# Where two modulation vectors are summed in a two-block diffusion transformer kernel

## The chip, the cores and the metric

The kernel runs on one core of a Trainium2 chip. The metric is the device time of one execution in microseconds (us). Three runs of the kernel before took 2163.9, 2153.99 and 2159.36 us; the median is 2159.36 us. One more execution was profiled; its own time is 2165.34 us and its traced span 2163.6 us.

The engines go by these names: PE is TensorE (matmuls; PEld are its weight loads), DVE is VectorE, ACT is ScalarE, POOL is GpSimd, and SP is SyncE, whose queue issues nearly all transfers of this kernel.

## The reference

Everything is fp32. 256 tokens and 256 context tokens of width 1024 pass through a first block of two layers and a second block of one layer; each layer is a mixer and then routed experts. The inputs of both halves are scaled and shifted, and their outputs gated, by six vectors that are computed from a condition:

```python
for layer in range(DEPTH):
    w_ada, b_ada = ada_w[layer], ada_b[layer]
    mod = (jax.nn.silu(c) @ w_ada + b_ada)[:, None, :]
    mod_c = (jax.nn.silu(c_ctx) @ w_ada + b_ada)[None, None, :]
    sh1, sc1, g1, sh2, sc2, g2 = jnp.split(mod, 6, axis=-1)
    csh1, csc1, cg1, csh2, csc2, cg2 = jnp.split(mod_c, 6, axis=-1)
    h = rms_norm(x, norm_mix_g[layer]) * (1.0 + sc1) + sh1
    ...
    x = x + g1 * y
    h2 = rms_norm(x, norm_ffn_g[layer]) * (1.0 + sc2) + sh2
    ...
    x = x + g2 * f[:b_ * t_].reshape(b_, t_, d_)
```

Here y is the mixer's output and f that of the experts. In layer 0 the mixer is an HGRN2 scan (4 heads) beside a differential attention (4 heads); the router picks 2 of 16 experts for each of the 512 tokens. Layer 1 has a windowed attention and the same kind of experts. The second block (another attention, a linear recurrence and 32 smaller experts) is not touched by the change.

The six vectors have the numbers 0 to 5 in the kernel: sh1, sc1, g1, sh2, sc2, g2. Vector 2 is the gate on the mixer's output, which is used when that output is projected; vector 5 is the gate on the experts' output, which is used from the experts' first scatter on.

## The kernel before, in words

`body` runs the six stages one after the other: `mixer0`, `moe(0)`, `mixer1`, `moe(1)`, `mixer2`, `moe(2)`. The code says what is computed and which tiles are shared; a scheduler then gives each engine one fixed row of instructions, mostly in the order in which the code reaches them, moved where it expects an operand late. An engine works through its row and waits at each instruction until its operands and its output buffer are free. SP does so too, so a transfer that waits for a page buffer holds up all transfers behind it.

**A modulation vector** is made by `ada(ps, parts, which, (v,))` in two halves (chunks) of 512 columns. For each, `ada_chunk` fetches two pages of 1 MB (4 of the 8 row blocks of the weight each), does 8 matmuls (L244, each 2 hardware instructions) into the four 32-row groups of one PSUM tile, and copies that to SBUF (L247: on DVE for the first chunk, on ACT for the second). `ada` then transposes the copy in 4 blocks (L265, 8 hardware instructions), and DVE adds up the four row groups (L267) and the bias (L269). Pages lie in 6 buffers, `pg`, that the weights of projections and experts share.

**mixer0** has a list of calls that lays the work of several heads in each other: H(h) is the next piece of HGRN2 head h, F(h) of attention head h, `a0(v)` and `a1(v)` are a modulation vector of layer 0 or 1. The last ones of before are H3, H3, H3, `a0(5)`, F3, F3, `a1(0)`, F3, `a1(2)`. A head's scan is a cascade of seven levels; at each, PE does 4 products (L453, 8 hardware instructions) and DVE three steps (L455, L457, L460). F3 ends in a softmax chain between PE (L546 scores, L563 transposes, L567 values), ACT and DVE. After the list, `router_start` folds vector 4 into the router's weights (L642), `as_row` spreads the gate over the partitions (L285), the output weights `even_w_out` (4 pages) are each split into a high and a low part (ACT L355, DVE L356), and `out_proj` multiplies (L366), gates (L581), adds (L584) and calls `router` for each of 4 token tiles: two transposes (L669, copies L670), the logits (L674) and L (L675).

**moe(0)** starts with the routing: DVE works out a mask `M` of the chosen experts; PE counts with it (L1349 to L1353), then spreads vector 5 by `as_row` (L285 again) and gathers tokens (L1499). Meanwhile ACT normalises the tokens (L1746, L1747) and POOL takes their low parts (L1748). At the end, `finish(1)` scatters the last 128 slots: for each of 8 half tiles, PE multiplies (L1567), DVE gates into a tile `t` (L1226; two buffers), and POOL or DVE adds to the tokens (L1571). Then every engine loads a count of overflowing blocks (`overflow`, L1868) and branches on it (L1874; the branch is taken past the body, as nothing overflows here). **mixer1** begins behind the branch with the norm of the tokens (ACT L295, transposes L327).

Of the kernel before, what the change touches and what calls it, by code (L numbers as in the profile page):

```python
# [20 lines left out]
P = 128  # L21
# [137 lines left out]
class K:  # L159
# [74 lines left out]
    def ada_chunk(self, ps, which, j, parts):  # L234

        nc, I = self.nc, self.I
        w = I["ada_w"][which] if which < 2 else I["w_ada_2"]
        s = 0 if which < 2 else 1
        wt = self.page(w[j])
        pa = self.t(ps, [P, 512], "ad", bufs=1) if which == 2 and j >= 4 else self.t(ps, [P, 512], "mm")  # L240
        for kk in range(2):
            for g in range(4):
                k = g + 4 * kk
                nc.tensor.matmul(out=pa[32 * g:32 * g + 32, :], lhsT=self.st[:, s, k, :],  # L244
                                 rhs=wt[:, k, :], start=(kk == 0), stop=(kk == 1))
        pt = self.w2(parts, [P, 512]) if which == 2 and j >= 4 else self.t(parts, [P, 512], "part")
        (nc.scalar.copy if j % 2 else nc.vector.tensor_copy)(out=pt, in_=pa)  # L247
        return pt
# [5 lines left out]
    def ada(self, ps, parts, which, vecs):  # L254
# [4 lines left out]
        for v in vecs:  # L259
            for half in (range(2) if isinstance(v, int) else (v[1],)):  # L260
                v = v if isinstance(v, int) else v[0]
                pt = self.ada_chunk(ps, which, 2 * v + half, parts)
                pc = self.t(ps, [P, 4, P], "tp")
                for b in range(4):
# [412 lines left out]
    def mixer0(self):  # L677
        tc, nc, I = self.tc, self.nc, self.I
        with ExitStack() as st:
# [53 lines left out]

            for f, v in ((H, 0), (H, 0), (H, 0), (H, 0), (a0, 2), (dval, 0), (F, 0), (F, 0), (H, 1), (F, 0), (H, 1), (H, 1), (H, 1), (a0, 4), (F, 1), (F, 1), (H, 2), (F, 1), (a1, 1), (H, 2), (H, 2), (H, 2), (a0, 3), (F, 2), (F, 2), (H, 3), (F, 2), (H, 3), (H, 3), (H, 3), (a0, 5), (F, 3), (F, 3), (a1, 0), (F, 3), (a1, 2)):
                f(v)
# [9 lines left out]
            for half in range(2):  # L745
                w = self.page(I["even_w_out"][half])
                wo.append(self.split(A, w, ("wh", "vt" if half else "wh"), (3, 1 if half else 3)))
            self.out_proj(ps, A, self.split_y(A, yT, ("hT0", "hT1")), wo, range(4), g1, 0, x0=x0)


# [949 lines left out]
    def moe(self, layer, plan, npages):  # L1700
# [6 lines left out]
        with ExitStack() as st:  # L1707
# [112 lines left out]
            for i, r in enumerate(rounds):  # L1820
# [4 lines left out]
                for p, ne in r:  # L1825
# [15 lines left out]
                    if layer == 1 and p == 1:  # L1841
                        self.early2(self.t(M, [P, 512], "t"))
            finish(1)
            slo, end, nbl = self.beyond(G, oh, info, nt, E, plan, ob)
            self.overflow(s, G, slo, end, nbl, E, ob, srcs, xtile)
# [144 lines left out]
```

## Time and profile before

| | |
|---|---|
| Median of three runs | 2159.36 us |
| The profiled execution: its time, its span | 2165.34 us, 2163.6 us |
| PE busy | 1946.4 us, 90% of the span |
| DVE, ACT, POOL busy | 941.3 (44%), 548.6 (25%), 248.0 us (11%) |
| Moved by transfers | 632.6 MB, 292 GB/s over the span |
| mixer0, and the routing after it | 0 to 464 us, to about 488 us |
| moe(0): experts, last scatter | about 488 to 1058 us, to 1073 us |
| mixer1, moe(1) | 1073 to about 1300 us, to about 1720 us |
| mixer2, moe(2) | to about 1900 us, to the end |

Busy shares are means over stages that differ: PE has no gap for long stretches and then waits for whole chains of other engines at the ends of a mixer and of the experts. What a piece of work costs is to be read at its place. A row of a timeline gives start and length in us, engine, line, operation, the tiles as output<-inputs, the shape, the count xN, and in brackets the idle time of the engine before it with what ended that. A row by line has the count, then busy us and mean ns of one, then the idle time before them and what ended it.

### The profile page before, as it was taken

How to read it: one execution, taken by the hardware profiler on the slowest of the kernel's cores; microseconds unless marked ns; L12 is line 12 of the kernel's file. 1: busy time of each engine (PE TensorE's matmuls, PEld its weight loads, DVE VectorE, ACT ScalarE, POOL GpSimd, SP SyncE). 2: the span in 40 equal slices, each digit the busy share in tenths (PEclk: the TensorE clock that was granted, in tenths of full speed). 3: DMA queues.
4: the chain of work that ended last, by engine and by line, in shares of the span. 5: the costliest groups of instructions: out<-in, count | busy, mean ns of one | idle time of the engine just before them, and what ended most of it. 6: DMA issues, size and time to landing. Idle time of an engine off the chain costs nothing. (4 is left out here: it accounts for less than half of the span.)

```text
span 2163.6 us, 29541 instructions
## 1 busy us (share of the span) xinstructions
PE 1946.4 (90%) x11795; PEld 1011.6 (47%) x11795; DVE 941.3 (44%) x2121; ACT 548.6 (25%) x1009; POOL 248.0 (11%) x203
## 2 busy tenths in 40 slices
PE   6999999969999999999799989998878869979986
PEld 3776665755443443333265563333322246655432
DVE  5536546454463234432456653222211155655533
ACT  4333433332221111110244431010100045521110
POOL 0000000020031012121300000101000011012212
PEclk9999999989999999999899999999999989989998
DMA  8423325335989998899554579999999976669997
GB/s 316 151 86 122 144 85 213 118 117 225 358 354 374 388 353 325 335 346 405 194 184 157 178 291 407 421 421 420 421 421 421 421 273 236 273 245 372 406 421 297
DMA packets 95587, 632.60 MB, mean 292 GB/s; under 512 B 15440, under 2 KB 17488, under 8 KB 19920
## 3 DMA queue, kind: packets, MB, share of 16 engines
q1 hardware_dynamic: 93888, 626.21, 73.5%
q10 hardware_dynamic: 1552, 4.39, 0.5%
q8 instruction: 97, 1.59, 0.3%
q14 instruction: 50, 0.41, 0.0%
HBM read 629.51 MB, written 1.05 MB: 291 GB/s over the span
## 5 line engine op out<-in xcount | busy, mean ns | idle before, releaser
L1602 PE MATMUL gu<-pg,xT 128*64 128x512 f32 (+1 forms) x2560 | 487.5, 597 | 19.5 <-DMA pg<-in_moe_gu_dram 19.5
L1635 PE MATMUL py<-pg,hT 128*64 128x512 f32 (+1 forms) x1280 | 258.3, 596 | 20.5 <-DVE hT L1619 17.4
L1602 PEld LDWEIGHTS gu<-pg,xT 128*64 128x64 f32 (+1 forms) x2560 | 133.1, 124 | 287.3 <-issue 231.1
L1571 POOL TENSOR_TENSOR xs<-xs,t 128x512 f32<-128x512 f32 x110 | 142.3, 1302 | 1089.5 <-DVE t L1226 1089.5
L1550 DVE SCALAR_TENSOR_TENSOR w<-py,swc,w 32x256 fp32r<-32x256 f32 (+3 forms) x142 | 95.5, 673 | 269.2 <-ACT w L1549 266.6
L375 PE MATMUL mm<-hT,wh 128*128 128x512 f32 (+1 forms) x672 | 194.2, 372 | 11.1 <-ACT w L431 5.1
L1549 ACT ACTIVATE w<-py,swc 32x256 fp32r<-32x256 f32 (+3 forms) x142 | 88.2, 621 | 403.5 <-PE py L1635 306.1
L1226 DVE TENSOR_TENSOR t<-x,w 128x512 f32<-128x512 f32 x156 | 105.8, 689 | 144.3 <-PE x L1567 122.0
L1226 DVE TENSOR_TENSOR hid<-hid,gu 128x512 f32<-128x512 f32 (+2 forms) x52 | 32.8, 631 | 296.8 <-PE gu L1602 251.2
L375 PEld LDWEIGHTS mm<-hT,wh 128*128 128x128 f32 x672 | 120.2, 194 | 44.6 <-issue 12.0
L1635 PEld LDWEIGHTS py<-pg,hT 128*64 128x64 f32 (+1 forms) x1280 | 77.7, 124 | 133.4 <-issue 75.6
L1567 PE MATMUL x<-w,S 128*128 128x512 f32 x312 | 115.1, 450 | 21.5 <-DVE t L1226 10.3
L375 PE MATMUL mm<-hT,pg 128*128 128x512 f32 (+1 forms) x336 | 123.8, 370 | 0.6 <-DVE pg L356 0.6
L1499 PEld LDWEIGHTS x<-oh,h 128*128 128x128 f32 x704 | 91.6, 189 | 55.9 <-issue 32.4
L1499 PE MATMUL x<-oh,h 128*128 128x256 f32 (+2 forms) x704 | 111.6, 292 | 5.7 <-DVE t L1226 2.7
L1612 ACT ACTIVATE hid<-gu 128x512 f32<-128x512 f32 (+1 forms) x41 | 24.4, 596 | 349.7 <-PE gu L1602 326.5
L1666 PE MATMUL gu<-pg,xT 128*32 128x256 f32 (+1 forms) x1024 | 101.6, 405 | 11.4 <-DMA pg<-in_moe_gu_dram 11.4
L1606 PE MATMUL gu<-pg,xT 128*32 128x512 f32 x640 | 111.6, 593 | 0.0
L1502 ACT ACTIVATE xT<-x,ac 128x256 f32<-128x256 f32 (+2 forms) x88 | 48.3, 549 | 217.1 <-PE x L1499 217.0
L1567 PEld LDWEIGHTS x<-w,S 128*128 128x128 f32 x312 | 50.7, 193 | 106.7 <-issue 31.7
L356 DVE TENSOR_TENSOR pg<-pg,wh 128x1024 fp32r<-128x1024 f32 (+1 forms) x74 | 89.1, 1213 | 22.9 <-ACT wh L355 22.5
L366 PE MATMUL mm<-wh,hT 128*128 128x512 f32 (+2 forms) x320 | 96.1, 380 | 1.8 <-ACT part L247 0.7
(499 smaller groups left out, 2582.2 us busy)
## 6 DMA issues: line engine op xcount, KB each, us to landing
pg<-in_moe_gu_dram SPq DMA_DIRECT2D x320, 1024.0 KB, 9.0
pg<-in_moe_d_dram SPq DMA_DIRECT2D x160, 1024.0 KB, 10.2
pg<-in_ada_w_dram SPq DMA_DIRECT2D x48, 1024.0 KB, 7.0
pg<-in_w_ada_dram SPq DMA_DIRECT2D x24, 1024.0 KB, 5.3
pg<-in_w0b_dram SPq DMA_DIRECT2D x8, 1024.0 KB, 6.2
pg<-in_w_dram SPq DMA_DIRECT2D x6, 1024.0 KB, 6.0
pg<-in_w0a_dram SPq DMA_DIRECT2D x4, 1024.0 KB, 8.5
pg<-in_w0c_dram SPq DMA_DIRECT2D x4, 1024.0 KB, 5.0
```

The source lines that it names most:

```text
L356: nc.vector.tensor_tensor(out=u[:, k:k + m], in0=x[:, k:k + m], in1=t[:, k:k + m].bitcast(F32), op=ALU.subtract)
L366: self.nc.tensor.matmul(out=pm, lhsT=hT[i][:, k, t * P:(t + 1) * P], rhs=w[j][:, k, c0:c0 + n], start=(m == 0), stop=(m == len(ops) - 1))
L375: self.nc.tensor.matmul(out=pm, lhsT=w[i][:, k, c0:c0 + P], rhs=hT[j][:, k, t0:t0 + nt], start=(m == 0), stop=(m == len(ops) - 1))
L1226: self.nc.vector.tensor_tensor(out=out, in0=a, in1=b, op=op)
L1499: nc.tensor.matmul(out=px[:, w, :], lhsT=l_, rhs=r_, start=(i == 0), stop=(i == len(ops) - 1))
L1550: nc.vector.scalar_tensor_tensor(out=lo[o:o + m, c0:c0 + w], in0=x, scalar=wc[o:o + m, :], in1=h.bitcast(F32), op0=ALU.mult, op1=ALU.subtract)
L1567: nc.tensor.matmul(out=px, lhsT=S[0:m, t * P:(t + 1) * P], rhs=y[0:m, cols], start=(i == 0), stop=(i == len(parts) - 1))
L1571: (nc.vector if last and h else nc.gpsimd).tensor_tensor(out=o, in0=o, in1=x, op=ALU.add)
L1602: nc.tensor.matmul(out=o[q:q + m64, :], lhsT=x64[0][:, k, x64[1] + r:x64[1] + r + m64], rhs=w[:, 512 * g:512 * g + 512], **f)
L1606: nc.tensor.matmul(out=pq[32 * q:32 * q + 32, :], lhsT=x32[0][:, k, x32[1]:x32[1] + 32], rhs=wk[q // 2][:, 512 * (q % 2):512 * (q % 2) + 5 ...
L1635: nc.tensor.matmul(out=py[q:q + m64, :], lhsT=h64[:, b, 64 * g + r:64 * g + r + m64], rhs=w[:, kk, 512 * h:512 * h + 512], **f)
L1666: nc.tensor.matmul(out=pg[r * e:r * e + r, 256 * i:256 * i + 256], lhsT=xT[:, k, c0 + r * e:c0 + r * e + r], rhs=ws[e][:, k, :], start=(k ...
```

## The change

Two calls move. `a0(5)` leaves its place between H3 and F3 and is called at the end of `mixer0`, after the output projection; vector 5 is needed by `as_row` in the routing. `a1(2)` leaves the end of the list and is called in `moe(0)` after the last scatter; vector 2 of layer 1 is needed at the end of `mixer1`. For layer 1's vector 2 (chunks j = 4 and 5) the PSUM tile is now `gu0` (one buffer, the experts' gate product), the SBUF tile is `t` (the scatter's two buffers), and the transposes' PSUM tile `tp` has one buffer.

```diff
-        pa = self.t(ps, [P, 512], "ad", bufs=1) if which == 2 and j >= 4 else self.t(ps, [P, 512], "mm")
+        if which == 1 and j in (4, 5):
+            pa = self.t(ps, [P, 512], "gu0", bufs=1)
+        else:
+            pa = self.t(ps, [P, 512], "ad", bufs=1) if which == 2 and j >= 4 else self.t(ps, [P, 512], "mm")
...
-        pt = self.w2(parts, [P, 512]) if which == 2 and j >= 4 else self.t(parts, [P, 512], "part")
+        if which == 1 and j in (4, 5):
+            pt = self.t(parts, [P, 512], "t")
+        else:
+            pt = self.w2(parts, [P, 512]) if which == 2 and j >= 4 else self.t(parts, [P, 512], "part")
...
-                pc = self.t(ps, [P, 4, P], "tp")
+                pc = self.t(ps, [P, 4, P], "tp", bufs=1) if which == 1 and v == 2 else self.t(ps, [P, 4, P], "tp")
...
-            for f, v in (..., (H, 3), (H, 3), (H, 3), (a0, 5), (F, 3), (F, 3), (a1, 0), (F, 3), (a1, 2)):
+            for f, v in (..., (H, 3), (H, 3), (H, 3), (F, 3), (F, 3), (a1, 0), (F, 3)):
                 f(v)
...
             self.out_proj(ps, A, self.split_y(A, yT, ("hT0", "hT1")), wo, range(4), g1, 0, x0=x0)
+
+            a0(5)
...
             finish(1)
+            if layer == 0:
+
+                self.ada(ps, M, 1, (2,))
             slo, end, nbl = self.beyond(G, oh, info, nt, E, plan, ob)
```

In the changed kernel the lines stand 3 to 11 lower: L244 is L247, L247 is L253, L265 is L271, L366 is L372, L546 is L552, L563 is L569, L567 is L573, L669 is L675, L674 is L680, L1349 is L1357, L1567 is L1575, L1868 is L1879, L1874 is L1885.

PE in the softmax chain of F3, before (mm and pg are a modulation vector's PSUM tile and page; two chunks of `a1(2)` are the tiles mm_2906 and mm_2929):

```order
L244 MATMUL mm_2867<-pg_2865,st 32x512 x3
L244 MATMUL mm_2906<-pg_2902,st 32x512 x4
L244 MATMUL mm_2906<-pg_2904,st 32x512 x4
L244 MATMUL mm_2929<-pg_2925,st 32x512 x4
L546 MATMUL lv_2746<-w_580_2703,w_575_2668 128x512
L546 MATMUL lv_2756<-w_580_2703,w_575_2668 128x512
L244 MATMUL mm_2929<-pg_2927,st 32x512
L563 MATMUL tp_2735<-cst,w_586_2717 128x128 x4
L244 MATMUL mm_2929<-pg_2927,st 32x512 x3
L567 MATMUL o_2711<-dv_338,w_595_2740 128x128 x4
L546 MATMUL lv_2780<-w_580_2703,w_575_2668 128x256
L546 MATMUL lv_2790<-w_580_2703,w_575_2668 128x256
```

The same place after (wh and pg on L372 are the parts of a page of output weights, hT those of the mixer's output):

```order
L247 MATMUL mm_2821<-pg_2819,st 32x512 x3
L372 MATMUL mm_2961<-wh_2923,hT_667_2951 128x512
L372 MATMUL mm_2961<-pg_2924,hT_667_2951 128x512
L372 MATMUL mm_2961<-wh_2923,hT_668_2952 128x512
L372 MATMUL mm_2961<-wh_2923,hT_667_2951 128x512
L372 MATMUL mm_2961<-pg_2924,hT_667_2951 128x512
L372 MATMUL mm_2961<-wh_2923,hT_668_2952 128x512
L372 MATMUL mm_2961<-wh_2923,hT_667_2951 128x512
L372 MATMUL mm_2961<-pg_2924,hT_667_2951 128x512
L552 MATMUL lv_2700<-w_568_2657,w_563_2622 128x512
L552 MATMUL lv_2710<-w_568_2657,w_563_2622 128x512
L372 MATMUL mm_2961<-wh_2923,hT_668_2952 128x512
```

The matmuls of `a1(2)` are gone, and products of the output projection stand between the scores instead.

PE at the end of mixer0, before (tp and lv belong to the router of the last token tile):

```order
L366 MATMUL mm_3336<-pg_3038,hT_691_3043 128x512
L366 MATMUL mm_3336<-vt_3037,hT_692_3044 128x512
L669 MATMUL tp_3371<-cst,pg_70 128x128 x4
L669 MATMUL tp_3377<-cst,pg_70 128x128 x4
L674 MATMUL lv_3383<-rwa_668_2966,w_730_3364 128x16 x8
L1349 LDWEIGHTS ones_b
L1349 MATMUL x_3459<-M_3457,ones_b 128x16
```

The same place after:

```order
L372 MATMUL mm_3244<-vt_2945,hT_668_2952 128x512
L675 MATMUL tp_3279<-cst,pg_70 128x128 x4
L247 MATMUL mm_3305<-pg_3301,st 32x512 x4
L247 MATMUL mm_3305<-pg_3303,st 32x512
L675 MATMUL tp_3285<-cst,pg_70 128x128 x4
L247 MATMUL mm_3305<-pg_3303,st 32x512 x3
L247 MATMUL mm_3328<-pg_3324,st 32x512
L680 MATMUL lv_3291<-rwa_644_2874,w_706_3272 128x16 x8
L247 MATMUL mm_3328<-pg_3324,st 32x512 x3
L247 MATMUL mm_3328<-pg_3326,st 32x512
L271 MATMUL tp_3316<-cst,part_3314 128x128 x4
L247 MATMUL mm_3328<-pg_3326,st 32x512 x3
```

`a0(5)` (the tiles mm_3305 and mm_3328) stands around the router's transposes and logits: nine of its sixteen products ahead of the logits, the rest and the transposes of both halves behind them and ahead of the count L1357.

PE at the end of moe(0), before:

```order
L1567 MATMUL x_7658<-w_1462_7473,S_7463 128x512
L1567 MATMUL x_7664<-w_1461_7472,S_7463 128x512
L1567 MATMUL x_7664<-w_1462_7473,S_7463 128x512
L1567 MATMUL x_7670<-w_1461_7472,S_7463 128x512
L1567 MATMUL x_7670<-w_1462_7473,S_7463 128x512
L1868 TENSOR_LOAD nbl_7697
L1874 COMPARE_AND_BRANCH
L1853 MATMUL x_7713<-cst,slo_7701 128x128 x4
```

The same place after (the first half of `a1(2)` is gu_1503, the second gu_1509; the first's products stand between the scatter's, further up):

```order
L1575 MATMUL x_7612<-w_1449_7426,S_7417 128x512
L1575 MATMUL x_7612<-w_1450_7427,S_7417 128x512
L1575 MATMUL x_7618<-w_1449_7426,S_7417 128x512
L1575 MATMUL x_7618<-w_1450_7427,S_7417 128x512
L1575 MATMUL x_7624<-w_1449_7426,S_7417 128x512
L1575 MATMUL x_7624<-w_1450_7427,S_7417 128x512
L271 MATMUL tp_7645<-cst,t_7643 128x128 x4
L247 MATMUL gu_1509_7657<-pg_7653,st 32x512 x4
L247 MATMUL gu_1509_7657<-pg_7655,st 32x512 x4
L271 MATMUL tp_7668<-cst,t_7666 128x128 x4
L1879 TENSOR_LOAD nbl_7697
L1885 COMPARE_AND_BRANCH
```

The transposes of the first half, all products of the second half and its transposes stand between the last scatter product and the load of the count. On DVE the copy of the first half stands behind the last gating step of the scatter; on ACT the copy of the second half stands ahead of the count's load. The branch is the last of each engine's row in this stage, so everything behind it, mixer1 first, comes after.

On SP, the four pages of `a0(5)` are now behind those of `even_w_out`, and those of `a1(2)` behind the last pages of the experts' gate and up weights, ahead of `w1`. Four pages of `a1(0)` are the only modulation pages left between F3's weights and `even_w_out`.

## Rows read from the trace of the kernel before

**Rows 1.** By stretch: start:end, length, busy of each engine, PE clock, DMA.

```profile
core 0: us, PE busy (x) PEld busy (x) DVE busy (x) ACT busy (x) POOL busy (x), PEclk, DMA share, GB/s
0.00:464.00 464.00, 420.14 (x2179) 299.96 (x2179) 238.27 (x548) 176.11 (x307) 18.48 (x24) 0.97 0.42 155
385.00:412.00 27.00, 26.26 (x146) 22.60 (x144) 13.34 (x31) 13.91 (x27) 1.01 (x1) 0.81 0.28 96
464.00:488.00 24.00, 8.76 (x70) 8.34 (x71) 22.56 (x80) 11.92 (x16) 9.25 (x4) 0.64 0.17 61
1065.00:1073.00 8.00, 3.50 (x7) 1.67 (x6) 5.16 (x8) 0.00 (x0) 3.56 (x3) 0.50 0.01 2
```

**Rows 2.** Timeline of TensorE, 329 to 349 us: start, length, engine, line.

```profile
330.12 1.49 PE L453 MATMUL lv<-w,w 128*128 128x128 f32 x8
345.79 1.13 PE L453 MATMUL lv<-w,w 128*128 128x128 f32 x8
348.42 0.79 PE L453 MATMUL lv<-w,w 128*128 128x128 f32 x5
```

**Rows 3.** By line, PE: 332-342, 359.5-361.5, 364.1-381.5 and 408-411 us.

```profile
L244 PE MATMUL mm<-pg,st 128*32 128x512 f32 x32 | 5.9, 601 | 0.0
...
L265 PE MATMUL tp<-cst,part 128*128 128x128 f32 x8 | 1.3, 280 | 0.0
...
L244 PE MATMUL mm<-pg,st 128*32 128x512 f32 x64 | 10.6, 611 | 1.8 <-DMA pg<-in_ada_w_dram 1.8
...
L265 PE MATMUL tp<-cst,part 128*128 128x128 f32 x8 | 1.2, 277 | 0.0
```

**Rows 4.** Timeline of TensorE, 357 to 385 us.

```profile
365.74 2.78 PE L244 MATMUL mm<-pg,st 128*32 128x512 f32 x24
377.05 1.82 PE L244 MATMUL mm<-pg,st 128*32 128x512 f32 x2
384.28 0.51 PE L366 MATMUL mm<-pg,hT 128*128 128x512 f32 x1 [1.36 <-DVE pg L356]
```

**Rows 5.** Timeline of SyncE (the transfers' queue), 326 to 382 us.

```profile
335.71 32.32 SPq L191 DMA_DIRECT2D pg<-in_ada_w_dram  x8
368.56 12.27 SPq L191 DMA_DIRECT2D pg<-in_even_w_out_dram  x4
```

**Rows 6.** Timeline of all engines, 455 to 492 us.

```profile
467.57 9.25 POOL L1748 TENSOR_TENSOR h<-w,h 128x1024 fp32r<-128x1024 f32 x4 [5.39 <-ACT h L1747]
467.68 2.27 DVE L1226 TENSOR_TENSOR goh<-goh,gohi 128x16 f32<-128x16 f32 x1
474.64 2.26 DVE L1226 TENSOR_TENSOR M<-oh 128x64 bf16<-128x64 f32 x1
476.95 0.28 PE L1349 MATMUL x<-M,ones_b 128*128 128x16 bf16 x4 [13.16 <-DVE M L1226]
477.35 5.59 PE L285 MATMUL x<-cst,ac 128*128 128x128 f32 x32
```

**Rows 7.** Timeline of all engines, 1047 to 1092 us.

```profile
1071.53 0.69 DVE L1226 TENSOR_TENSOR t<-x,w 128x512 f32<-128x512 f32 x1 [1.15 <-POOL pg L1571]
1072.26 0.69 DVE L1571 TENSOR_TENSOR pg<-pg,t 128x512 f32<-128x512 f32 x1
1073.32 1.06 ACT L295 ACTIVATE w<-xs 128x1024 f32<-128x1024 f32 x1 [13.31 <-PEq L1874]
1080.88 1.11 PE L327 MATMUL tp<-cst,w 128*128 128x128 f32 x4 [0.59 <-DVE w L333]
```

**Rows 8.** By line (ns min/median/max): the count's load, its branch, the two copies.

```profile
L1868 PEldq TENSOR_LOAD <-nbl x1: 486/486/486, 1069.2 to 1069.2; - x1
...
L1874 PEldq COMPARE_BRANCH  x3: 423/445/3292, 1069.8 to 2154.8; - x3
...
L247 DVE COPY part<-mm x14: 680/692/693, 14.1 to 1237.1; 128x512 f32<-128x512 f32 x14
L247 ACT COPY part<-mm x14: 565/585/594, 21.8 to 1240.3; 128x512 f32<-128x512 f32 x14
```

More of the change, by code (lines that the diff above doesn't have):

```diff
@@ L732, in a1 @@
                 self.ada(ps, parts, 1, (v,))
-            for f, v in ((H, 0), (H, 0), (H, 0), (H, 0), (a0, 2), (dval, 0), (F, 0), (F, 0), (H, 1), (F, 0), (H, 1), (H, 1), (H, 1), (a0, 4), (F, 1), (F, 1), (H, 2), (F, 1), (a1, 1), (H, 2), (H, 2), (H, 2), (a0, 3), (F, 2), (F, 2), (H, 3), (F, 2), (H, 3), (H, 3), (H, 3), (a0, 5), (F, 3), (F, 3), (a1, 0), (F, 3), (a1, 2)):
+            for f, v in ((H, 0), (H, 0), (H, 0), (H, 0), (a0, 2), (dval, 0), (F, 0), (F, 0), (H, 1), (F, 0), (H, 1), (H, 1), (H, 1), (a0, 4), (F, 1), (F, 1), (H, 2), (F, 1), (a1, 1), (H, 2), (H, 2), (H, 2), (a0, 3), (F, 2), (F, 2), (H, 3), (F, 2), (H, 3), (H, 3), (H, 3), (F, 3), (F, 3), (a1, 0), (F, 3)):
                 f(v)
```

## The prediction, made before the changed kernel was run

> **What bounds the kernel now.** The busy times by stretch come first. In mixer0 PE works 420.14 of 464 us [rows 1]: a matmul taken out there shortens the path unless it only filled a wait. In the routing behind it PE works 8.76 of 24 us while DVE works 22.56, and in the last 8 us of the scatter PE works 3.50 at a clock of 0.50, that is 1.2 of 2.4 GHz [rows 1]. So both vectors leave a place where PE is short for places where PE idles. The second view is the timeline, at the places they leave and at the places they go to: for each new place the reader should ask whether the work runs beside the chain that ends the stage, or becomes part of it. The answers differ. The experts' matmuls between the two new places keep their work; their start only shifts.
>
> **What leaves the H3 cascade: `a0(5)`, about -4 us.** Its 32 hardware matmuls are busy 5.9 us and its 8 transposes 1.3 us [rows 3]. They stand between the seven levels of head 3's scan, so not all of that is gained. The first and the last level begin at 330.12 and 348.42 us: six steps in 18.30 us, of which the last, between 345.79 and 348.42, took 2.63 without such a matmul inside [rows 2]. Six steps of 2.63 are 15.78, so 2.5 us go; with the transposes behind the cascade, 3.8. F3's projection takes the free place, which shortens what follows it a little. The ends are 2.5 (the transposes too only filled a wait) and 5.9 + 1.3 = 7.2 us (PE is the limit throughout). I take -4, next to the cascade's own step.
>
> **What leaves F3's softmax chain: `a1(2)`, about -8 us.** 64 matmuls of two vectors are busy 10.6 us between 364.1 and 381.5 [rows 3]; half of them, 5.3, go, and 1.2 us of transposes [rows 3]. With them goes what their pages cost: PE waited 1.8 us for one [rows 3], and 1.36 us for the split of the output weights [rows 4], whose four pages are issued only from 368.56 us on, behind eight modulation pages [rows 5]. Sum: 5.3 + 1.2 + 1.8 + 1.4 = 9.7. Against it stands a new wait: products of the output projection now fill the chain earlier, and SP sends the third page only when `a1(0)` has read its third, in the same 365 us or so. The old wait of 1.36 is the nearest row; I take some 1.7, hence -8. Behind the chain, PE works 26.26 of 27 us at a clock of 0.81 [rows 1]; at full clock that stretch would be (1 - 0.81) x 27 = 5 us shorter. Whether denser filling brings that, no row says. It makes the favourable end -13. The other end is -1: the chain of ACT and DVE steps sets the pace and PE's freed time turns into idle time.
>
> **What the routing takes on: `a0(5)`, about +1 us.** PE idles 13.16 us before its count [rows 6]. 16 matmuls at full clock take 2.78 x 16/24 = 1.85 us [rows 4], so two halves and their transposes, some 5 us, and twice that at half clock, fit into that gap; vector 5 is first read by `as_row` at 477.35 [rows 6]. Three things are not covered. Nine of sixteen products and DVE's copy of the first half (0.69 us [rows 8]) stand ahead of the last tile's logits and L; four small DVE steps stand in the chain to M; and on ACT the second copy, which waits for PE's last product, stands ahead of the casts that feed POOL. The first two delay M by 0 to 3 us. The third moves POOL's four steps. While these ran (9.25 us), DVE's step on 16 columns at 467.68 took 2.27 us and M took 2.26 [rows 6]: each small step waits out one of POOL's. A later POOL lets some of those steps through before it, and holds up the ones behind M instead. Hence -2 to +3; I take +1. The Trainium skill, page "SBUF — State Buffer", section "SBUF: two separate sides", says that DVE steps with two SBUF inputs and GpSimd steps take a shared port pair by an exclusive lock, held for a whole instruction. The trace agrees, and by that rule each of POOL's four steps still finds one DVE step to hold, so the sum stays at +1. The four more MB of transfers find a queue that is used 0.17 in these 24 us [rows 1].
>
> **What the end of moe(0) takes on: `a1(2)`, about +8 us.** This is the step that can undo the rest. The branch behind the scatter needs all engines, and PE reaches it only after the second half's transposes, because `gu0` has one buffer. Before, the last gating step ended at 1071.53 + 0.69 = 1072.22 us; PE's branch lasted from 1069.8 for 3.292 us, to 1073.1, and mixer1's first step came at 1073.32, ended by PE's branch [rows 7, 8]. After, from 1072.22: DVE copies half one, 0.69; four transposes, 1.3/2 = 0.65 [rows 3], or 1.11 at half clock [rows 7]; 16 products, 1.85, or at the ratio of the transposes 3.2 (a lone pair took 1.82 us in a stretch of lowered clock [rows 4]); ACT copies half two, 0.585 [rows 8]; four transposes; the count's load, 0.486; the branch, 0.423 as in the shortest of three, or 3.292 [rows 8]; four handovers, an estimate of 0.05 each. At full clock with a short branch that is 0.69 + 0.65 + 1.85 + 0.585 + 0.65 + 0.486 + 0.423 + 0.2 = 5.5, ending at 1077.7: +4.6. At half clock it is 7.8: +6.9. The long branch adds 2.87: up to +9.8. In those 8 us the clock was 0.50 [rows 1], so I take half clock and, between the two branches, +8. The first half's products stand between the scatter's and find PE idle there, half of 8 us; they cost 0 to 1. DVE's last addition (0.69 at 1072.26 [rows 7]) now runs beside this. The added pages push `w1`'s back, on a queue with nothing else to do (DMA 0.01 [rows 1]).
>
> The Trainium skill, page "Runtime: NRT & Kernel Launch", section "Instruction fetch mechanics", says that a taken branch whose target is not in the window of fetched instructions stalls for the fetch. One of three branches here lasted 3.292 us, the others under 0.45 [rows 8], which fits; by that rule the wait starts anew behind the moved work and the end would cost nearer +9.8, the sum -1.
>
> **The sum.** -4 - 8 + 1 + 8 = -3 us. On the profiled execution, 2165.34 us, that is 2162.3. That execution lies 5.98 us above the median; on the median, 2159.36, the forecast is 2156 us. All favourable ends together give -7.2 - 13 - 2 + 4.6 = -17.6, all others -2.5 - 1 + 3 + 11 = +10.5.
>
> **Rivals.**
>
> *The scan and the chain set the pace, and the join costs in full: slower.* If F3's chain of DVE and ACT steps is the limit, PE's freed time there becomes idle time. For it: PE shared the chain with other filler before, and has output products to fill in after. Against it: PE had no wait inside the chain but for transfers. Then -4 - 1 + 1 + 9 = +5, 2164 us. It decides when mixer0 shrinks by less than some 9 us.
>
> *The clock comes back and the join is cheap: clearly faster.* If mixer0's end runs denser at full clock (-13) and the branch behind the join is short at full clock (+4.6): -4 - 13 + 0.5 + 4.6 = -12, 2147 us. For it: the 5 us at a lowered clock are there to be had. Against it: of `a1(2)` only transposes stood in that stretch; the rest of its work stays.
>
> *The moved pages come late, so that the change doesn't hide what it says.* SP now sends the pages of `a0(5)` ahead of the first experts'. If these reach PE late, moe(0) starts later by about one page's spacing in that queue, 32.32/8 = 4 us [rows 5], on top: 2160 us. Against it: 24 us with transfers 0.17 busy [rows 1] lie ahead of the first use.
>
> **How the numbers follow.** Forecast 0.56; paced chain 0.17; clock and cheap join 0.20; late pages 0.07. What a measurement of this kernel can tell from no change is about 0.5%, 10.8 us. The favourable rival passes -10.8 in most of its cases and the forecast in a few: faster 0.21. The paced chain passes +10.8 only with all its ends, late pages only with a slow join: slower 0.09. The rest, 0.70, is within 0.5%. The range runs from 2146, just beyond the favourable rival's 2147, to 2166, beyond the paced chain's 2164; 2 in 10 lie outside. The forecast's own range is 2150 to 2162.
>
> **What would show it.** PE's levels in H3 should step by 2.6 us, and the part up to the last output product should end some 12 us earlier. In F3 the output products should run between the scores with at most one wait for a split. PE's count should come as late after the last output product as before, within 3 us. At the end of moe(0), from the last gating step to mixer1's first norm there should be 8 to 10 us instead of 1.1, with copy, transposes, products, copy, transposes in it one after the other. The forecast is wrong if mixer0 shortens by under 8 us or over 17, if the join costs under 4 or over 11, or if moe(0) between them changes its length by more than 2.

## The result: 0.7% slower, and where the time went

The changed kernel takes 2172.89 us (median of five runs, 2171.23 to 2180.32) against 2159.36 us. The two medians are 0.63% apart; the ratio on record is 1.0074, with a 95% interval of 1.0057 to 1.0092. A second set of runs of it beside 23 of the kernel before gave 1.0063 [1.0047, 1.0080], 14 us. The forecast was 2156 us and the range ended at 2166: the prediction was wrong, in sign and by more than its range allowed. The profiled execution of the changed kernel took 2171.23 us, with a span of 2169.5.

The page of the changed kernel, its first part: busy time of each engine, share of the span, instructions.

```profile
PE 1951.0 (90%) x11795; PEld 1012.9 (47%) x11795; DVE 939.6 (43%) x2121; ACT 548.7 (25%) x1009; POOL 247.6 (11%) x203
```

Nothing but places has changed: the busy times are those of before within 5 us, PE's 4.6 us longer. The next rows are its stretches, with the columns of [rows 1]: mixer0 to its last output product, the router of the last tile up to the count, the rest of the routing, and the end of moe(0) from the last expert's work to the branch.

```profile
0.00:450.86 450.86, 405.08 (x2075) 294.04 (x2076) 232.94 (x533) 172.32 (x301) 17.94 (x23) 0.97 0.38 135
450.86:463.50 12.64, 9.36 (x67) 4.46 (x65) 7.92 (x34) 7.04 (x10) 0.69 (x2) 1.00 0.98 381
463.50:487.48 23.98, 14.26 (x100) 13.26 (x101) 19.50 (x61) 9.70 (x15) 9.50 (x4) 0.79 0.33 135
1053.43:1078.07 24.64, 14.54 (x56) 4.78 (x56) 10.80 (x23) 1.94 (x3) 6.09 (x4) 0.83 0.16 52
```

Taken against the first trace of before, mixer0 is 7 us shorter, as if most of the forecast had come true. It had not, as further traces of the *unchanged* kernel show; and 2.8 of the 7 us lie ahead of H2's last level, where nothing was edited. A table of stages, worked out from the timelines of each trace (from the start of one row to the start of the next; H2's last level counts from the start of its last product, and the output products, the logits and the gating step count at their ends; the last column is described with the experiments):

| us | before, 4 traces | changed, 2 traces | both vectors' products left out |
|---|---|---|---|
| H2's last level to H3's first | 53.7 to 56.4 | 58.0, 57.7 | 57.5 |
| H3's first level to F3's rotation | 35.0 (all four) | 30.4, 31.7 | 31.7 |
| F3's rotation to its last transposes | 43.4, 36.7, 40.0, 38.8 | 40.9, 38.6 | 38.8 |
| from there to the last output product's end | 50.1 (all four) | 51.1, 52.0 | 51.0 |
| to the last tile's logits | 5.2 to 6.2 | 5.7, 5.7 | 6.3 |
| logits to the count | 13.2 | 6.5, 6.5 | 13.2 |
| count to the first expert's product | 15.0 | 24.0, 23.6 | 15.0 |
| last gating step's end to mixer1's norm | 1.1 to 1.5 | 10.3, 10.3 | 1.5 |
| that norm to mixer1's first projection | 16.8 | 17.4, 17.4 | 16.8 |

**H3's cascade** did what was expected. The timeline of TensorE in the changed kernel, two levels: the step is 2.61 us, with 1.48 us of waiting for DVE, where the last step before was 2.63 [rows 2].

```profile
342.41 1.13 PE L459 MATMUL lv<-w,w 128*128 128x128 f32 x8 [1.48 <-DVE w L463]
345.02 1.13 PE L459 MATMUL lv<-w,w 128*128 128x128 f32 x8 [1.48 <-DVE w L463]
```

**F3's chain** did not. First the second trace of before, TensorE: the filler (work that keeps TensorE busy while the chain is on other engines) is the vectors' products, which wait 0.94 us for a page. The last row is the first output product that needs F3's output, which waits 0.18 us.

```profile
372.33 1.06 PE L244 MATMUL mm<-pg,st 128*32 128x512 f32 x8 [0.94 <-DMA pg<-in_ada_w_dram]
388.80 3.66 PE L642 MATMUL lv<-rw,ac 128*128 128x16 f32 x32
392.31 2.75 PE L285 MATMUL lv<-cst,ac 128*128 128x128 f32 x22
404.48 0.50 PE L366 MATMUL mm<-wh,hT 128*128 128x512 f32 x1 [0.18 <-ACT hT L609]
```

Then the changed kernel at the same place, TensorE and after that ScalarE and VectorE; the last row is TensorE's second scores in `neither`, a kernel of the next section.

```profile
362.64 1.13 PE L552 MATMUL lv<-w,w 64*128 64x512 f32 x4
368.76 2.37 PE L552 MATMUL lv<-w,w 64*128 64x512 f32 x4 [1.60 <-ACT w L559]
387.34 4.16 PE L648 MATMUL lv<-rw,ac 128*128 128x16 f32 x32
403.56 0.50 PE L372 MATMUL mm<-wh,hT 128*128 128x512 f32 x1 [2.48 <-ACT hT L615]
...
364.14 2.00 ACT L361 CAST wh<-pg 128x1024 fp32r<-128x1024 f32 x2 [2.20 <-DMA pg<-in_even_w_out_dram]
366.04 0.58 ACT L253 COPY part<-mm 128x512 f32<-128x512 f32 x1
367.93 0.69 ACT L559 ACTIVATE w<-lv,mx 128x512 f32<-128x512 f32 x1
...
366.63 1.22 DVE L362 TENSOR_TENSOR pg<-pg,wh 128x1024 fp32r<-128x1024 f32 x1
369.03 1.21 DVE L616 TENSOR_TENSOR hT<-xs,hT 128x1024 fp32r<-128x1024 f32 x1
...
368.53 1.79 PE L551 MATMUL lv<-w,w 64*128 64x512 f32 x4 [1.36 <-ACT w L558]
```

The pages of output weights now stand eight pages earlier in the queue. ACT casts two halves of one, 2.00 us, *ahead of* the first exponential (L559), on which the chain waits; DVE's parts of the splits (1.22 and 1.21 us) stand between its own steps of the chain. PE's second scores then wait 1.60 us for that exponential and take 2.37 us; at a granted clock of 1.00 they still take 1.79, as `neither` shows, since their second half waits for the second exponential. And at the end of F3 there are no output products left to fill in, as they were used up: PE idles 2.48 us before the first one that needs F3's output.

**The routing**: POOL's four steps, once ahead of M [rows 6], lie behind it. All engines of the changed kernel:

```profile
463.35 9.64 POOL L1756 TENSOR_TENSOR h<-w,h 128x1024 fp32r<-128x1024 f32 x4 [8.57 <-ACT h L1755]
463.50 0.26 PE L1357 MATMUL x<-M,ones_b 128*128 128x16 bf16 x4 [2.58 <-DVE M L1234]
465.91 2.40 DVE L1234 TENSOR_TENSOR cmp<-key 128x256 f32<-128x256 f32 x1
468.80 2.00 DVE L1234 TENSOR_TENSOR cmp<-cst,pos 128x256 f32<-128x256 f32 x1
470.72 2.31 DVE L1240 TENSOR_SCALAR cap<-pos 128x16 f32<-128x16 f32 x1
```

The count comes 6.65 us sooner after the logits, and what follows it takes 9 us longer: three of DVE's steps behind M now last 2.0 to 2.4 us and a fourth 1.43, as four of 2.3 to 2.4 us, among them `goh` and M, did before.

**The join** at the end of moe(0), all engines of the changed kernel; it answers to [rows 7, 8]. The last row, from the view of line L1885, is TensorE's branch in ns.

```profile
1067.06 0.69 DVE L1234 TENSOR_TENSOR t<-x,w 128x512 f32<-128x512 f32 x1 [1.15 <-POOL pg L1579]
1067.66 0.68 DVE L253 COPY t<-gu 128x512 f32<-128x512 f32 x1
1068.49 1.09 PE L271 MATMUL tp<-cst,t 128*128 128x128 f32 x4 [3.00 <-DVE t L253]
1069.51 3.63 PE L247 MATMUL gu<-pg,st 128*32 128x512 f32 x16
1073.26 0.58 ACT L253 COPY t<-gu 128x512 f32<-128x512 f32 x1 [17.66 <-PE gu L247]
1073.89 0.66 PE L271 MATMUL tp<-cst,t 128*128 128x128 f32 x4 [0.76 <-ACT t L253]
1078.07 1.06 ACT L301 ACTIVATE w<-xs 128x1024 f32<-128x1024 f32 x1 [4.23 <-PEq L1885]
...
L1885 PEldq COMPARE_BRANCH  x1: 3332/3332/3332, 1074.5 to 1074.5; - x1
```

Copy, transposes, products (3.63 us, at a granted clock of 0.53), copy, transposes and the branch stand one after the other, as the prediction laid them out: 10.3 us where 1.1 was.

### The profile page after: what moved, and what is told of

It reads as the page before. It is cut to its first block, busy times and chain, and to the rows that moved or that the text cites. A ratio compares the mean times of both kernels' runs of the same rounds, so it can differ in the third digit from the quotient of the medians.

```text
span 2169.5 us, 29542 instructions
## 1 busy us (share of the span) xinstructions
PE 1951.0 (90%) x11795; PEld 1012.9 (47%) x11795; DVE 939.6 (43%) x2121; ACT 548.7 (25%) x1009; POOL 247.6 (11%) x203
## 5 line engine op out<-in xcount | busy, mean ns | idle before, releaser
L1610 PE MATMUL gu<-pg,xT 128*64 128x512 f32 (+1 forms) x2560 | 487.6, 597 | 18.5 <-DMA pg<-in_moe_gu_dram 18.4
L1643 PE MATMUL py<-pg,hT 128*64 128x512 f32 (+1 forms) x1280 | 258.3, 596 | 21.4 <-DVE hT L1627 17.4
L1575 PE MATMUL x<-w,S 128*128 128x512 f32 x312 | 112.3, 441 | 20.1 <-DVE t L1234 9.6
L372 PE MATMUL mm<-wh,hT 128*128 128x512 f32 (+2 forms) x320 | 97.1, 384 | 3.9 <-ACT hT L615 2.5
L1575 PEld LDWEIGHTS x<-w,S 128*128 128x128 f32 x312 | 49.0, 188 | 106.0 <-issue 31.7
```

The source lines that it names most:

```text
L372: self.nc.tensor.matmul(out=pm, lhsT=hT[i][:, k, t * P:(t + 1) * P], rhs=w[j][:, k, c0:c0 + n], start=(m == 0), stop=(m == len(ops) - 1))
L1575: nc.tensor.matmul(out=px, lhsT=S[0:m, t * P:(t + 1) * P], rhs=y[0:m, cols], start=(i == 0), stop=(i == len(parts) - 1))
L1610: nc.tensor.matmul(out=o[q:q + m64, :], lhsT=x64[0][:, k, x64[1] + r:x64[1] + r + m64], rhs=w[:, 512 * g:512 * g + 512], **f)
L1643: nc.tensor.matmul(out=py[q:q + m64, :], lhsT=h64[:, b, 64 * g + r:64 * g + r + m64], rhs=w[:, kk, 512 * h:512 * h + 512], **f)
```

## The experiments

**The halves apart.** The diff of each against the kernel before, the repeated long list cut; `only_a12` also has the changed kernel's edits of tiles.

```diff
 only_a05
-  ..., (H, 3), (a0, 5), (F, 3), (F, 3), (a1, 0), (F, 3), (a1, 2)):
+  ..., (H, 3), (F, 3), (F, 3), (a1, 0), (F, 3), (a1, 2)):
...
+            a0(5)
 only_a12
-  ..., (a1, 0), (F, 3), (a1, 2)):
+  ..., (a1, 0), (F, 3)):
...
+            if layer == 0:
+                self.ada(ps, M, 1, (2,))
 neither
-  ..., (H, 3), (a0, 5), (F, 3), (F, 3), (a1, 0), (F, 3), (a1, 2)):
+  ..., (H, 3), (b0, 5), (F, 3), (F, 3), (a1, 0), (F, 3), (b1, 2)):
```

`neither` leaves out the products, copies, transposes and pages of both vectors, at either place; only their bias is written. `again` is the changed kernel once more.

> Only vector 5 of layer 0 moves to the end of mixer0; vector 2 of layer 1 stays in mixer0. Theory of places (each vector costs and gains where it lies, as the two traces show): mixer0 shorter by about 4 us (the cascade's levels at 2.6 us), the stretch from the last output product to the first expert product longer by about 3 us, the join behind moe(0) as before: 2158 us, within 3 us of before. Rival (something between runs, such as the clock, makes up most of the measured +13 us, not the two places): the time lies 5 us or more above before although the trace shows neither place longer.

> Only vector 2 of layer 1 moves to the end of moe(0); vector 5 stays between H3 and F3. Theory of places: mixer0 shorter by 3 to 4 us, the join 9 us later against the last gating step: +6 us, about 2165. Rival (between runs): as the whole change, +13 us, with a trace that shows +6 or less.

> Both vectors are left out at their old places: only their bias is written, so the gates lack the condition. This prices what mixer0 can gain. Theory of places: mixer0 shorter by the 7.3 us that the changed kernel's trace shows, or up to 2 more, routing and join as before: 2150 to 2152 us. Rival (F3's chain does not set the pace, PE does): mixer0 shorter by 12 to 13 us as the prediction's terms had it, 2147 us.

> The changed kernel once more, for the spread of its times and a second trace. Theory of places: the same stretches within 1 us (mixer0 -7.3, join +9.2), and a time 6 to 16 us above before. Rival (between runs): its stretches differ from the first trace by several us at a place where the two engines meet by chance, such as the routing with its four GpSimd steps.

Measured on one chip, against 23 runs of before (median 2158.45 us): `only_a05` 2162.23 us, 1.0012 [0.9997, 1.0027]; `only_a12` 2170.11 us, 1.0052 [1.0035, 1.0069]; `neither` 2159.88 us, 1.0010 [0.9998, 1.0023]; `again` 2172.62 us, 1.0063. The expectations for `only_a12` (+6 us) and `neither` (2150 to 2152 us) failed, as both counted on a shorter mixer0. So about four fifths of the loss belong to `a1(2)`, whose place in F3 gave nothing back. The strongest of these is `neither`: with both vectors' work gone from everywhere, the kernel is not faster than before. So the gain of taking them out of mixer0 is about zero, whatever they cost at the new places. What `neither` leaves out changes the values that later stages see, but no gain was lost there: from mixer1's first projection to the end its trace takes 1074.1 us, those of before 1072.4 to 1081.2.

**How much one trace of before can be trusted.** The kernel before, unchanged, traced twice more:

> The kernel before once more, for a second trace, since its runs lie between 2153.8 and 2169.2 us and its first trace is at 2165.3. If the first trace is typical, every stage repeats within 1 us. If one place varies from run to run, a run at 2155 to 2160 us shows it: most likely the routing behind mixer0, where DVE met four GpSimd steps (13.2 us from the logits to the count), which would then be some 6 us shorter.

> The same, a third trace of the kernel before: as the second.

They took 2161.33 and 2169.81 us; nine runs of before on that chip had a median of 2157.93. The table above has their stages: F3's stretch took 43.4, 36.7, 40.0 and, in a fourth trace (`before_again`, below), 38.8 us, with the same instructions in the same order. The routing, which the expectation had suspected, kept its 28.1 us from the logits to the experts. Here are windows of TensorE (start:end, length, busy, clock, DMA share, GB/s): the first trace of before, the second, and the changed kernel.

```profile
375.00:390.00 15.00, 13.40 (x58) 0.77 0.65 246
390.00:405.00 15.00, 14.93 (x92) 0.77 0.08 20
...
375.00:390.00 15.00, 13.21 (x76) 1.00 0.53 218
390.00:405.00 15.00, 14.24 (x101) 1.00 0.52 187
...
360.00:375.00 15.00, 13.31 (x55) 0.83 0.58 203
390.00:405.00 15.00, 11.26 (x62) 0.74 0.29 103
```

The first trace ran part of F3 at the lower of the two clock levels (a mean of 0.77), the second ran at 1.00 throughout. The 43.4 us from which the prediction subtracted 8 held some 7 us of low clock that the next trace did not have. The changed kernel has a low stretch as well, and in 390 to 405 us PE is busy only 11.26 of 15 us, for want of filler. Over 375 to 405 us the mean granted clock is 0.83 to 0.89 in all seven traces without `a1(2)` in F3 and with nothing delayed; in the six that keep it, it is 0.77 to 1.00, and 1.00 in two of them.

**What sets the pace in F3.** Two kernels are the changed one with one thing delayed: in `split_late` the splits of the output weights and of y on ACT and DVE wait for the last softmax step of F3; in `prod_late` only PE's output products wait, for the last value product.

```diff
 split_late
-                wo.append(self.split(A, w, ("wh", "vt" if half else "wh"), (3, 1 if half else 3)))
+                with self.after(self.lastA), self.after(self.lastD):
+                    wo.append(self.split(A, w, ("wh", "vt" if half else "wh"), (3, 1 if half else 3)))
...
 prod_late
+            y = self.split_y(A, yT, ("hT0", "hT1"))
+            with self.after(self.lastP):
+                self.out_proj(ps, A, y, wo, range(4), g1, 0, x0=x0)
```

> As the changed kernel, but ACT and DVE split the output weights and the mixer's output only behind the last step of F3's softmax, so that neither the splits nor the output products that need them stand in the chain. Measured between F3's second rotation product (L511) and the transposes behind its values (L417): 40.9 and 38.6 us in the two traces of the changed kernel, 36.7 in the best trace of before. Theory (the splits on ACT and DVE stand in the chain and lengthen it): 28 to 32 us. Rival (the chain's own latency is 36 us): 35 us or more. The whole run says little, as the products that leave come later.

> As the changed kernel, but only the output products wait until F3's last values are multiplied; the splits stay where they are. PE has then almost nothing beside the chain. Same stretch. Theory (splits): 36 to 40 us, as in the changed kernel, although some 42 products of 0.23 us are gone from it. Rival (PE's products, in order ahead of scores and transposes, are what lengthens it): 28 to 32 us, as without the splits.

They took 2184.17 and 2188.76 us in one execution each (before on that chip: 2159.16), both longer than the changed kernel. The stretch that the expectations name took 39.9 and 45.5 us: the 28 to 32 hoped for in `split_late` did not come, and both fell to the lower clock. What can still be read is F3's first step, chosen after the result. TensorE in `split_late` (first three rows) and in `prod_late`:

```profile
362.39 1.13 PE L552 MATMUL lv<-w,w 64*128 64x512 f32 x4
369.66 2.08 PE L573 MATMUL o<-dv,w 128*128 128x128 f32 x8 [0.68 <-ACT w L571]
375.07 1.11 PE L569 MATMUL tp<-cst,w 128*128 128x128 f32 x4 [2.18 <-DVE w L566]
...
372.06 2.74 PE L552 MATMUL lv<-w,w 64*128 64x512 f32 x4 [3.42 <-ACT w L559]
386.02 1.12 PE L569 MATMUL tp<-cst,w 128*128 128x128 f32 x4 [3.96 <-DVE w L566]
```

From the rotation to the middle of the first values it is 10.8 us in `split_late`, 16.7 in `prod_late`, 16.4 in `again`, and 13.1 in `only_a05`, which keeps `a1(2)` in F3. Where the clock was 1.00 up to there, it is 16.3 to 16.4 us in five traces without `a1(2)` and 13.1 to 14.4 in five with it. So the splits ahead of the exponential make the first step long. PE's products do little: taking them away left 16.7 us, of which some 1 us is due to the lowered clock, an estimate from transposes of 1.11 us instead of 0.60 and values of 2.08 instead of 1.16 (`prod_late` against `neither`). Moving the splits gains 5.6 us; 3.3 of these came in with the output weights' splits, the rest belongs to those of y, which stand ahead of the exponential in `only_a05` too. But the gain doesn't last: the rest of `split_late`'s chain runs at half clock (its value products take 2.08 us), and the late splits are paid behind F3, where the output projection's stretch is 60.8 us instead of 51. `prod_late` idles and runs at a clock of 0.50, that is 1.2 GHz, through 375 to 405 us:

```profile
375.00:390.00 15.00, 7.65 (x30) 0.50 0.42 139
390.00:405.00 15.00, 14.54 (x66) 0.50 0.01 3
```

**Can the gain be had?** `after_late1` is the changed kernel with the splits behind the *first* softmax step only, so that output products can still fill the others. `gap_late1` does the same with `a0(5)` left at its old place and `a1(2)` put at the end of mixer0, where `a0(5)` stands in the changed kernel, so that there is no join.

```diff
 after_late1
-            self.lastA = nc.scalar.copy(out=aT, in_=tp)
+            i = nc.scalar.copy(out=aT, in_=tp)
+            self.lastA = i if ti == 0 else self.lastA
...
 gap_late1 (against before; the delay of the splits as above)
-  ..., (a1, 0), (F, 3), (a1, 2)):
+  ..., (a1, 0), (F, 3)):
...
+            a1(2)
```

> As the changed kernel, but ACT and DVE start the splits of the output weights and of the mixer's output behind the first of F3's four softmax steps, not ahead of it. Theory (the splits lengthen the chain's first step): rotation to first values 10.8 us as without splits, against 16.4, and if the later steps keep 18.5 us and the output projection its 51 to 52, mixer0 is 5 us shorter than in the changed kernel: 2167 us. Rival (the splits only move to the next step): the four steps together keep 35 us and the time stays at 2172.

> Vector 5 stays between H3 and F3, vector 2 of layer 1 goes to the end of mixer0, whose routing has idle time on PE and does not need it, and the splits start behind F3's first step. Nothing is added at the end of moe(0). Theory of places: F3 5 us shorter than in the changed kernel, its cascade as before, the routing 2 to 3 us longer as measured for vector 5, the join as before: 2157 to 2160 us, the same as before within 0.2%. Rival (the chain's time only moves): 2162 us or more.

2171.55 us, 1.0053 [1.0036, 1.0071], and 2163.78 us, 1.0020 [1.0007, 1.0032]. The first step is 10.1 and 10.6 us, as hoped; but from there to the end of the last values it is 27.0 and 27.7 us, where the seven traces without `a1(2)` in F3 and with nothing delayed have 18.5 to 19.0, and the whole of F3 40.7 and 41.8, no less than without. So the rival of each expectation came out: the time only moves. In a window of `after_late1` the granted clock is 0.64 (0.59 in that of `gap_late1`), which goes with it; `only_a05`, which keeps `a1(2)` and had 0.83 over 375 to 405 us, has 23.2.

```profile
375.00:390.00 15.00, 12.77 (x62) 0.64 0.00 1
```

**The join.** Three versions of it. `behind` keeps `a0(5)` as changed, but calls `a1(2)` in mixer1 behind its norm and transposes, with mixer0's kinds of tiles; `two_tiles` gives the second half its own PSUM tile; `ahead` calls the vector before the last scatter.

```diff
 behind (in mixer1, behind h_transposed; the call in moe(0) and the edits of tiles are undone)
+            self.ada(ps, parts, 1, (2,))
 two_tiles (against the changed kernel)
-            pa = self.t(ps, [P, 512], "gu0", bufs=1)
+            pa = self.t(ps, [P, 512], f"gu{j % 2}", bufs=1)
 ahead (against the changed kernel)
-            finish(1)
             if layer == 0:
                 self.ada(ps, M, 1, (2,))
+            finish(1)
```

> As the changed kernel, but vector 2 of layer 1 is computed in mixer1 behind its first norm and transposes, with that stage's own tiles, instead of ahead of the branch. Theory of places: the join is as before (1.1 us from the last gating step to mixer1's first norm instead of 10.3), PE idles at that place for 10 of 17 us, so mixer1 grows by at most 3 us: 6 to 9 us below the changed kernel, 2163 to 2166 us, about +6 against before. Rival (what is summed anywhere near the stage's start costs its full time): mixer1 grows by 8 us or more, as slow as the changed kernel.

> As the changed kernel, but the second half of vector 2 has the other PSUM tile gu1, so that its products need not wait for the copy of the first half. Theory of places (the join's cost is a chain through one PSUM tile at half clock): the join shrinks by about 3 to 4 us, the products of the second half; 2168 us. Rival (the cost is the wait of PE's branch, which begins anew): the join shrinks by under 1 us.

> As the changed kernel, but vector 2 is called ahead of the last scatter, so that its products, copies and transposes lie between the first of the scatter's steps and PE reaches the count's load behind the last scatter product. Theory of places: the join from the last gating step to mixer1's first norm is 1.1 us again instead of 10.3, and the scatter grows by 3 to 6 us, since its steps wait for tiles and for DVE: 2164 to 2168 us. Rival (the work costs the same wherever it lies at this end, since the chain of scatter, vector and branch is one): as the changed kernel, 2172 us.

`behind` 2168.03 us, 1.0047 [1.0034, 1.0061]; `two_tiles` 2171.18 us, 1.0058 [1.0045, 1.0072]; `ahead` 2167.06 us, 1.0048 [1.0031, 1.0064]. From the last gating step to the norm there are -0.6, 7.9 and 1.5 us, so the join goes where the work goes; in `two_tiles` it shrinks by 2.4 us instead of the expected 3 to 4, as 6 of the second half's 16 products still stand in it. But in `behind` mixer1's first projection then comes 4.9 us later after the norm, more than the 3 expected, and in `ahead` the scatter takes 18.6 us instead of 13.7, from its first product to the last gating step. From that step to the projection `behind` takes 21.1 us, before 17.9 to 18.4 and the changed kernel 27.7. So the work costs 3 us in mixer1 (with the short branch below counted in), 5 in the scatter, and 9.5 where it is joined. Two rows, from `behind` (TensorE's branch, ns) and from `two_tiles` (TensorE's products that still stand in the join):

```profile
L1883 PEldq COMPARE_BRANCH  x1: 353/353/353, 1068.8 to 1068.8; - x1
...
1072.71 1.81 PE L247 MATMUL gu<-pg,st 128*32 128x512 f32 x6
```

**The routing.** `dve_copy` is `only_a05` with the copy of the vector's second half on DVE, so that ACT's casts for POOL need not wait for it.

```diff
-        (nc.scalar.copy if j % 2 else nc.vector.tensor_copy)(out=pt, in_=pa)
+        (nc.scalar.copy if j % 2 and (which, j) != (0, 11) else nc.vector.tensor_copy)(out=pt, in_=pa)
```

> As the kernel in which only vector 5 moved, but its second half is copied by DVE instead of ACT, so that ACT's casts for GpSimd's four steps are not behind it. Theory (the late ACT copy moves GpSimd's steps behind M and onto the slot arithmetic): logits to count 13 us again instead of 6.5, count to first expert product 15 instead of 24, together 2 us less than with the ACT copy. Rival (the sum of the two is what the four steps cost, wherever they lie): together the same 30.7 us within 0.5.

2158.5 us in one execution (before on that chip: 2159.16). POOL's four steps are ahead of M again, and DVE's steps on `rk` alternate between held and free. All engines:

```profile
455.09 9.95 POOL L1750 TENSOR_TENSOR h<-w,h 128x1024 fp32r<-128x1024 f32 x4 [5.99 <-ACT h L1749]
453.94 0.69 DVE L247 COPY part<-mm 128x512 f32<-128x512 f32 x1 [0.82 <-PE mm L244]
455.20 2.60 DVE L1228 TENSOR_TENSOR rk<-sel 128x256 f32<-128x256 f32 x1
459.96 0.41 DVE L1228 TENSOR_TENSOR rk<-sel 128x256 f32<-128x256 f32 x1
466.86 0.28 PE L1351 MATMUL x<-M,ones_b 128*128 128x16 bf16 x4 [11.52 <-DVE M L1228]
```

From the logits to the first expert it is 15.55 + 14.50 = 30.1 us, against 30.7 in `only_a05`, 30.5 and 30.2 in the changed kernel's two traces and 28.1 before: 0.6 us of the hoped-for 2 came. But this doesn't show that the place of POOL's steps is free, since DVE's own copy, 0.69 us behind a wait of 0.82 for PE, now stands ahead of M too. What every trace has, wherever POOL's steps lie, is four held steps on DVE. The Trainium skill, page "SBUF — State Buffer", section "SBUF: two separate sides", has DVE's steps with two SBUF inputs (or in a mode that uses both ports) and GpSimd's steps wait for each other for a whole instruction; the trace agrees, as the same step on `rk` takes 2.60 us beside POOL and 0.41 us between. The changed kernel's `cap`, a step with one input, was held too (2.31 us); whether it uses such a mode, no row shows.

**A comparison of the kernel before with itself**, for the size of what can be told:

> The kernel before against itself, since its three traces so far (2161 to 2170 us) lie above the median of the runs it is compared with (2158 to 2159). If the comparison is even, the ratio is 1.000 within 0.002; if a kernel run under its own label is slower than as the one compared with, the ratio is 1.002 or more and all ratios here are too high by that.

0.9991 [0.9978, 1.0005], medians 2156.99 and 2158.87 us. A difference of 2 us is within what two equal kernels show. No version that was run is shown to be faster than the kernel before.

## Why the prediction was wrong, point by point

- **F3, predicted -8 us, is the step that failed.** Over four traces of before and two other kernels that keep `a1(2)` there (`only_a05`, `dve_copy`), it takes 86.1 to 93.5 us from F3's rotation to the last output product, 89.4 on the mean; over seven traces with `a1(2)` out and nothing else delayed (the changed kernel twice, `neither`, `only_a12`, `behind`, `two_tiles`, `ahead`) 89.8 to 92.9, 90.9 on the mean. That is +1.6, and +3.7 between the best of each. The terms of the sum were right as work: 5.3 us of products and 1.2 of transposes left. They were no gain because they had been filler, as `neither` shows. In their place came the output products, with splits on ACT and DVE ahead of the exponential, and the tail behind F3 lost its own filler, 1 to 1.9 us. The rival of the paced chain had named this place at -1; even that was too favourable.
- **One trace was taken for the kernel.** About 1 us of the -8 was read out of a stretch with a lowered clock: in the second trace of before the 64 products take 9.8 us instead of 10.6 and wait 1.2 instead of 1.8. I had set the 5.98 us by which the profiled execution lay above the median aside as an offset at the end. The other three traces of before are 3.4 to 6.7 us shorter in the very stage at issue, so much of that offset lay in F3. By the prediction's own sign (mixer0 shorter by under 8 us) even the first pair of traces, with 7.3, spoke against it.
- **H3, predicted -4**: the cascade and its tail gave -3.2 and -4.6, so term and mechanism were right. But the stretch before H3's first level is 57.5 to 58.9 us in eleven traces without `a0(5)` in H3, and 53.7 to 56.4 in six with it: 2.5 on the mean goes back. The pages of F3 and of the output weights come earlier there too, and the order changes from F2 on. That this is the cause was only argued, not shown.
- **The routing, predicted +1**: +2.0 to +2.4 from the logits to the experts, and 0.5 ahead of the logits. It lies within the given -2 to +3. That a held step behind M replaces one before it was right, but the parts came out otherwise: M was to come up to 3 us later and PE's count within 3 us of its old distance from the last output product, and the count came 6.1 us sooner after that product, with 9 us lost behind it. That the two nearly cancel, as the term had it, is in part luck.
- **The join, predicted +8**: +9.0 (10.3 against a mean of 1.3 in four traces of before), and +0.5 behind it. The chain was the forecast one; the branch was the long one (3.332 us) and the products took 3.63 us where 3.2 was put. The Trainium skill, page "Runtime: NRT & Kernel Launch", section "Instruction fetch mechanics", gives a stall to a taken branch outside the fetched window; by that rule the prediction's +9.8 was the likely end. The traces fit, with 3.3 to 3.9 us in all of them but `behind`, where it is 0.353. Why it is short there, no run shows.
- **The sum** by these: +2.5 - 3.9 + 1.6 + 2.7 + 9.5 = +12.4 us, against a measured 13.6 to 16. `only_a12` alone gives 1.6 + 9.5 = 11.1 and measures 1.0052, 11.2 us; `only_a05` gives 2.5 - 3.9 + 2.7 = 1.3 and measures 2.6, with an interval that holds it. In the same way `behind` gives 5.9 and `ahead` 8.1 us, and they measure 10.1 and 10.4. Each of these sums comes out short, the two last by 2 to 4 us; one likely reason, not shown, is that the four traced executions of before (2162.8 us on the mean) lie some 4 us above the medians of its runs, so that its stages look too long. moe(0) between its ends kept its length (566.6 and 566.7 us from the first expert's product to the scatter's first), and its pages were not late: that rival fell.

What stays open is what starts a lowered-clock stretch in one execution and not in the next, and why both kernels that delay the splits by one step had one in 375 to 390 us. Nor is it told apart how much of F3's +1.6 is the longer first step and how much the clock.

## What to carry to other kernels

A matmul that stands in another engine's latency chain can be filler: before a gain is booked for taking it out, ask what takes its place, what *that* needs from the engines of the chain, and where that was filler before. A test that leaves the work out altogether costs one run and gives the ceiling of any such move; here it was zero. And where stages differ by 7 us between executions of the same program, a sum of 3 us is not to be made against one trace.

## What the hardware showed that was not expected

In F3 the same program ran at a granted clock of 1.00 in one execution and 0.77 in another over 375 to 405 us, worth about 7 us of 2160. With the splits late, or the output products late, the clock fell to 0.64 and 0.50 over 375 to 390 us, with PE busy 12.77 and 7.65 of 15 us; over the next 15 us of `prod_late` it stayed at 0.50 with PE busy 14.54. TensorE's branch at the end of moe(0) lasted 3.3 to 3.9 us in every trace but one, while the same branch on DVE took 72 ns and on ACT and GpSimd 45.
